# Expert-weight slots of a one-core transformer block: tiles of the front part kept as small rings, and a new order of slots

## The chip, the cores and the metric

The kernel runs on one core of a Trainium2 chip. The metric is device time in microseconds of one execution. Three timed runs of the kernel before took 698.36, 703.17 and 704.9 us, so the median is 703.17 us. The profiled execution took 699.28 us, of which 697.5 us lie between the first and the last instruction.

## The reference

One block over 256 tokens of width 1024. A normalised and modulated input goes through one projection into three mixers (an RWKV-7 recurrence, differential attention, block attention), their outputs through `w_out`, and the sum is added to `x`. Then comes a mixture of 32 experts with two levels of routing:

```
mod = cs @ ada_w + ada_b                      # 6 x 1024 modulation vectors
h   = rmsnorm(x, norm1_g) * (1 + sc1) + sh1
y_r, y_d, y_m = three mixers of (h @ w_in)
x   = x + g1 * (concat(y_r, y_d, y_m) @ w_out)
h2  = rmsnorm(x, norm2_g) * (1 + sc2) + sh2
# each token: best of 4 groups, then 2 of its 8 experts
x   = x + g2 * sum over chosen experts e of gate * (silu(h2 @ w1[e]) * (h2 @ w3[e])) @ w2[e]
```

All arrays are float32. The experts' weights are 32 x 3 x 2 MB = 201 MB. They are all read, whatever the routing.

## The kernel before

**Order of the work.** The front part (modulation, projections, mixers, `w_out`) comes first. The router follows, and then nine groups of experts: group 0 is experts 0 to 3, known beforehand; the numbers of the others come from a permutation `perm` that the router computes. For each group, `hidden` gathers the tokens, multiplies by `w1` and `w3` (output `h`), and `experts_out` multiplies by `w2` (output `yb`).

**Loads.** Every load is issued by SP, in one queue in order. `wtile` (L1173) hands out a place of 1 MB for each load of expert weights: a full expert takes two for `w1`, two for `w3`, two for `w2`, so there are 192 such tiles, 24 of them for group 0. In a group the order of tiles is first halves of `w1`, first halves of `w3`, second halves of `w1`, second halves of `w3`, then `w2`. L1170 sets from which ring each place is taken, and the list is gone through again and again; it has 20 places. I number the tiles 1 to 192 in that order; tile 21 takes the place of tile 1, and its load waits until TensorE has used tile 1 up. Tile 21 still belongs to group 0. SP's queue reaches `perm` (L1190) behind tile 24.

**Places.** `ringB` holds ten tiles. In the front part they are four tiles of `w_in` (`wR`), the recurrence's operands (KB, MA, ER, ta), `dqk` and `tb`; two of them are taken again for half of `w_out` (`rwo`). `ringA` holds two tiles (modulation and projection weights, later the other half of `w_out`). `ringC` holds eight, and is opened only when the pools of the front part are closed (L985 to L988). So tiles 1 to 12 go into places that come free within the front part, and 13 to 20 into `ringC`.

**Other tiles of the front part.** `ringF` (two places) holds the modulation weights (`ra`); its last four loads, `in_adaM`, are used by matmuls `ga`, which make the gate `g2`. The transposed input `hT` and the split weights `wp1` share one place, `wp0` has one of its own, and `hTl` and the mixers' output `mT` share another. All of these lie in the pool `fr`, which closes with the front part. The projection's matmuls `pt` are the last that read `wp0` and `wp1`.

**What sets the order.** The program is laid out by a scheduler that simulates it and places each instruction in its engine's queue when its operands and its place are there by the simulation. It also sets the order of SP's queue, within the order that `load_next` fixes for the front part's own loads.

Of the kernel before, what the change touches and what calls it, by code (L numbers as in the profile page):

```python
# [8 lines left out]
FT = mybir.dt.float32  # L9
FR = mybir.dt.float32r  # L10
# [8 lines left out]
S, D, NT = 256, 1024, 2  # L19
# [3 lines left out]
BIG = 1.0e30  # L23


NA, NB, NC, NF = 2, 10, 8, 2
PK, GROUPS = {}, {}


# [65 lines left out]
def build(tc, ctx, a):  # L95
# [4 lines left out]
    const = ctx.enter_context(tc.tile_pool(name="const", bufs=1))  # L100
    keep = ctx.enter_context(tc.tile_pool(name="keep", bufs=1))
    ringA = ctx.enter_context(tc.tile_pool(name="ringA", bufs=NA))
    dram = ctx.enter_context(tc.tile_pool(name="dram", bufs=1, space=bass.MemoryType.DRAM))
    small = ctx.enter_context(tc.tile_pool(name="small", bufs=2))
    front = ExitStack()
    fr = front.enter_context(tc.tile_pool(name="front", bufs=1))
    ringF = front.enter_context(tc.tile_pool(name="ringF", bufs=NF))
    att = ExitStack()
    at = att.enter_context(tc.tile_pool(name="att", bufs=1))
    rp = att.enter_context(tc.tile_pool(name="rwkv", bufs=1))  # L110
    ringB = ctx.enter_context(tc.tile_pool(name="ringB", bufs=NB, side="right", reuse_waits="tile"))
# [96 lines left out]
    def ahead(it, n):  # L208

        q = []  # L210
        for x in it:
            q.append(x)
            if len(q) > n:
                yield q.pop(0)
        yield from q
# [3 lines left out]
    A.activation(cs, c_("c"), AF.Silu)  # L219
    A.activation(csb, csb, AF.Silu)  # L220

    hT = fr.tile([128, 8, S], FT, name="hT", tag="hT")
    ssx = const.tile([128, NT], FT, name="ssx")
    rx = const.tile([128, NT], FT, name="rx")
    for t in range(NT):
# [69 lines left out]
    def pieces(specs):  # L295
        for i, s_ in enumerate(specs):
            for k, w in load_win(i, s_[1] - s_[0]):
                yield s_, k, w
# [3 lines left out]
    DM = ((896, 1408, dq[:, :, 0:512], 0), (1408, 1920, dq[:, :, 512:1024], 8), (1920, 2432, dv, None),  # L302
          (2432, 2944, mqk, 16), (2944, 3200, mv, None))

    wp = [fr.tile([128, 2, 2, 512], FR, name="wp0"), None]

    def split(it):

        for x, (s_, k, w) in enumerate(it):
            if x == 2:  # L310
                wp[1] = fr.tile([128, 2, 2, 512], FR, name="wp1", tag="hT")
            hi, lo = (wp[x // 2 % 2][:, x % 2, q, :w.shape[-1]] for q in range(2))
            A.copy(hi, w)  # L313
            V.tensor_sub(lo, w, hi)  # L314
            yield s_, k, hi, lo

    hTh = keep.tile([128, 8, S], FR, name="hTh", tag="xn")
    hTl = fr.tile([128, 8, S], FR, name="hTl", tag="hTl")
    src = ahead(split(ahead(pieces(DM), 6)), 2)


# [178 lines left out]
    mt_ = []  # L500

    def mT():

        if not mt_:
            assert 2944 in done
            mt_.append(fr.tile([128, 8, S], FT, name="mT", tag="hTl"))
        return mt_[0]


# [10 lines left out]
    def rwkv():  # L520
# [222 lines left out]
        for j in range(2):  # L743
            A.activation(yr[:, j, :], pz[:, j].rearrange("p n t -> p (n t)"), AF.Identity, bias=c_("lnb")[:, j:j + 1],
                         scale=c_("lng")[:, j:j + 1])
        V.tensor_add(yr, yr, bon)
        V.tensor_mul(mT()[:, 0:2, :], yr, zg.rearrange("p (j t) -> p j t", j=2))
        done.add(("j", 0))
        done.add(("j", 1))
# [87 lines left out]
    def apply_M(i, aTs):  # L837
        po = bankt("pm_")[:, :256]
        for x, aT in enumerate(aTs):
            h = 2 * (i - 4) + x  # L840
            q = HQ[x]
            vh = mv[:, :, 64 * h:64 * h + 64]
            T.matmul(po[q, 0:128], vh[:, 0, :], aT[:, 0, :], start=True, stop=True, tile_position=(0, 64 * x))
            T.matmul(po[q, 128:256], vh[:, 0, :], aT[:, 1, :], start=True, stop=False, tile_position=(0, 64 * x))
            T.matmul(po[q, 128:256], vh[:, 1, :], aT[:, 2, :], start=False, stop=True, tile_position=(0, 64 * x))
        A.copy(mT()[:, 2 + i, :], po)

    def out_D(h2):

        rd = at.tile([128, 2, NT], FT, name="rd", bufs=2)  # L850
        rstd_of(rd.rearrange("p h t -> p (h t)"), ssd[:, 2 * h2:2 * h2 + 2, :].rearrange("p h t -> p (h t)"), 128, 1e-6,
                [128, 4])
        for t in range(NT):
            o3 = od[:, t, 256 * h2:256 * h2 + 256].rearrange("p (h e) -> p h e", h=2)
            V.tensor_mul(o3, o3, rd[:, :, t:t + 1].to_broadcast([128, 2, 128]))
        yield 0.6
        p = bankl("od").rearrange("p (h t q) -> p h t q", h=2, t=NT)
        for hh in range(2):
            h = 2 * h2 + hh
            for t in range(NT):  # L860
                T.transpose(p[:, hh, t, :], od[:, t, 128 * h:128 * h + 128], ident)
        j = slice(2 + 2 * h2, 4 + 2 * h2)
        pq = p.rearrange("p h t q -> p h (t q)")
        A.activation(mT()[:, j, :], pq, AF.Copy, scale=sub)
        done.add(("j", 2 + 2 * h2))
        done.add(("j", 3 + 2 * h2))
# [121 lines left out]
    ringC = ctx.enter_context(tc.tile_pool(name="ringC", bufs=NC, reuse_waits="tile"))  # L988
# [178 lines left out]
        A.copy(grow, pg.rearrange("p c t q -> p c (t q)"))  # L1167


    seq = [ringB] * NB + [ringA] * NA + [ringC] * NC  # L1170
    cnt = [0]

    def wtile():  # L1173
# [298 lines left out]
```

## Time and profile before

| what | value |
|---|---|
| median of three runs | 703.17 us |
| profiled execution | 699.28 us |
| its span | 697.5 us |
| TensorE busy | 582.4 us (84%) |
| VectorE busy | 255.7 us (37%) |
| moved by DMA | 249.36 MB, mean 358 GB/s |
| TensorE's mean granted clock | 0.946 |

The busy shares are averages over a front part of some 230 us, in which TensorE and VectorE have the work, and the experts' part after it, in which the same 16 DMA engines move almost nothing but expert weights. A busy TensorE in that second part includes matmuls whose ends are modelled, so the DMA row is read beside it.

### The profile page before, as it was taken

What the parts mean: (1) busy time and instruction counts of PE and PEld (TensorE: products, weight loads), DVE (VectorE), ACT (ScalarE), POOL (GpSimd) and SP (SyncE); (2) the same over time, 40 slices, a digit from 0 to 9 for tenths busy, and PEclk for the clock granted to TensorE, in tenths of its full rate; (3) what the DMA queues carried; (4) which work ended last, traced back from release to release, by engine and by line L of the source; (5) the groups of instructions that cost most, each with busy time, mean ns of one, the idle gap of its engine ahead of it and who ended that gap; (6) DMA issues with size and microseconds to landing.
All of it is one profiled execution on the core that took longest, in us unless ns stands there. A gap on an engine that the chain in (4) does not pass through costs nothing. (4 is left out here: it accounts for less than half of the span.)

```text
span 697.5 us, 9345 instructions
## 1 busy us (share of the span) xinstructions
PE 582.4 (84%) x3612; PEld 271.3 (39%) x3612; DVE 255.7 (37%) x683; ACT 135.1 (19%) x299; POOL 28.1 (4%) x39
## 2 busy tenths in 40 slices
PE   2967999999989697998867999996886688788676
PEld 1856887675444543433213243431221115121112
DVE  5777998667535742321301122130030013002002
ACT  3366444544331412101001010100000002000000
POOL 2223200000000000000000000000000000000000
PEclk9997999999989898999989999998998999899799
DMA  9991775477665699999999999999999999999996
GB/s 356 422 356 64 295 278 184 152 295 275 235 231 191 264 420 419 421 419 420 422 419 420 424 420 420 420 420 422 420 419 422 419 409 420 420 420 421 420 389 235
DMA packets 42678, 249.36 MB, mean 358 GB/s; under 512 B 4220, under 2 KB 10244, under 8 KB 14984
## 3 DMA queue, kind: packets, MB, share of 16 engines
q1 hardware_dynamic: 42632, 248.74, 88.5%
q8 instruction: 29, 0.48, 0.3%
q14 instruction: 17, 0.14, 0.1%
HBM read 247.66 MB, written 1.06 MB: 357 GB/s over the span
## 5 line engine op out<-in xcount | busy, mean ns | idle before, releaser
L69 PE MATMUL h<-rmoe,xT 128*32 128x512 f32 (+1 forms) x1024 | 191.3, 662 | 39.3 <-DMA rmoe<-in_moe_w 39.3
L69 PE MATMUL yb<-rmoe,aTm 128*32 128x512 f32 (+2 forms) x544 | 104.2, 579 | 14.2 <-DMA rmoe<-in_moe_w 9.9
L69 PEld LDWEIGHTS h<-rmoe,xT 128*32 128x32 f32 (+1 forms) x1024 | 44.2, 122 | 171.5 <-issue 90.5
L1256 DVE TENSOR_TENSOR ac<-ac,h 128x512 f32<-128x512 f32 x9 | 6.2, 688 | 168.3 <-PE h L69 167.7
L69 PEld LDWEIGHTS yb<-rmoe,aTm 128*32 128x32 f32 (+1 forms) x544 | 28.6, 113 | 82.8 <-issue 41.9
L1255 ACT ACTIVATE ac<-h 128x512 f32<-128x512 f32 x9 | 5.4, 597 | 255.2 <-PE h L69 255.1
L1291 DVE TENSOR_TENSOR yb<-yb,g2b 128x512 f32<-128x512 f32 (+1 forms) x19 | 12.6, 664 | 110.7 <-PE yb L69 110.7
L69 PE MATMUL pt<-wp,hTh 128*128 128x512 f32 (+1 forms) x160 | 51.3, 400 | 1.0 <-ACT wp L313 0.5
L69 PE MATMUL cb<-yb,ST 128*128 128x512 f32 (+1 forms) x76 | 40.3, 618 | 7.6 <-DVE x L1295 6.2
L69 PE MATMUL gx<-S,xn 128*128 128x128 f32 x288 | 40.3, 297 | 5.0 <-DVE S L85 2.2
L1295 DVE TENSOR_TENSOR x<-x,cb 128x512 f32<-128x512 f32 (+1 forms) x38 | 25.1, 660 | 50.6 <-PE cb L69 50.5
L69 PEld LDWEIGHTS gx<-S,xn 128*128 128x128 f32 x288 | 37.0, 207 | 15.6 <-issue 13.1
L1237 ACT ACTIVATE xT<-gx,sh,s2c 128x128 f32<-128x128 f32 x36 | 16.0, 456 | 94.1 <-DVE xT L1239 94.1
L69 PEld LDWEIGHTS pt<-wp,hTh 128*128 128x128 f32 x160 | 28.8, 195 | 9.3 <-issue 1.7
L69 PE MATMUL pt<-wp,hTl 128*128 128x512 f32 (+1 forms) x80 | 30.3, 381 | 0.0
L69 PE MATMUL op<-rwo,mT 128*128 128x512 f32 x64 | 30.3, 617 | 0.0
L313 ACT CAST wp<-rwin 128x512 fp32r<-128x512 f32 (+1 forms) x40 | 22.7, 576 | 29.3 <-PE pt L69 28.2
L69 PE MATMUL pr<-hT,rwin 128*128 128x256 f32 x112 | 25.2, 383 | 3.7 <-ACT hT L372 3.7
L314 DVE TENSOR_TENSOR wp<-rwin,wp 128x512 fp32r<-128x512 f32 (+1 forms) x40 | 26.5, 683 | 3.9 <-ACT wp L313 3.8
L69 PEld LDWEIGHTS cb<-yb,ST 128*128 128x128 f32 x76 | 11.6, 188 | 36.2 <-DVE x L1295 21.2
L1239 DVE TENSOR_SCALAR xT<-gx,s2c,sh 128x128 f32<-128x128 f32 x36 | 14.4, 408 | 27.3 <-PE gx L69 27.3
L69 PEld LDWEIGHTS pr<-hT,rwin 128*128 128x128 f32 x112 | 21.0, 191 | 7.8 <-ACT hT L372 4.9
(370 smaller groups left out, 558.8 us busy)
## 6 DMA issues: line engine op xcount, KB each, us to landing
rmoe<-in_moe_w SPq DMA_DIRECT2D x184, 1024.0 KB, 19.8
ra<-in_adaB SPq DMA_DIRECT2D x8, 1024.0 KB, 13.9
ra<-in_adaC SPq DMA_DIRECT2D x8, 1024.0 KB, 7.0
rwin<-in_winD SPq DMA_DIRECT2D x8, 1024.0 KB, 5.1
ra<-in_adaM SPq DMA_DIRECT2D x8, 1024.0 KB, 7.1
rwo<-in_w_out SPq DMA_DIRECT2D x4, 1024.0 KB, 8.0
rmoe<-in_moe_w SPq DMA_DIRECT2D x8, 512.0 KB, 17.1
rmoe<-in_moe_w SPq DMA_DIRECT2D x16, 256.0 KB, 5.7
```

Of the source, the lines that this page charges most:

```text
L69: return self._turn(self.engine.matmul(*ar, **kw))
L313: A.copy(hi, w)
L314: V.tensor_sub(lo, w, hi)
L1237: A.activation(xT[:, k, :], p[kk_ // 2][:, kk_ % 2, :], AF.Identity, bias=sh2[:, k:k + 1], scale=s2c[:, k:k + 1])
L1239: V.tensor_scalar(xT[:, k, :], p[kk_ // 2][:, kk_ % 2, :], s2c[:, k:k + 1], sh2[:, k:k + 1], op0=OP.mult, op1=OP.add)
L1255: A.activation(ac, hs[0], AF.Silu)
L1256: V.tensor_mul(ac, ac, hs[1])
L1291: V.tensor_mul(yb_[:, f], py_[c], g2b[:, f])
L1295: V.tensor_add(x2[:, t, f], x2[:, t, f], p)
```

## The change

The places of `hT`, `wp1` and `wp0` become `ringE` (two places), those of `hTl` and `mT` become `ringD` (one place), and `ringF` is moved out of the pools that close with the front part. All three rings stay open to the end, so the experts' tiles can use them. `ringC` shrinks from eight places to three, so there are still 20 places. The list that `wtile` goes through is written in another order: two of `ringB`, the two of `ringE`, the two of `ringF`, six of `ringB`, three of `ringC`, two of `ringA`, two of `ringB`, one of `ringD`. The diff, without its comments and blank lines:

```
-NA, NB, NC, NF = 2, 10, 8, 2
+NA, NB, NC, ND, NE_, NF = 2, 10, 3, 1, 2, 2
...
     ringA = ctx.enter_context(tc.tile_pool(name="ringA", bufs=NA))
+    ringD = ctx.enter_context(tc.tile_pool(name="ringD", bufs=ND))
+    ringE = ctx.enter_context(tc.tile_pool(name="ringE", bufs=NE_))
+    ringF = ctx.enter_context(tc.tile_pool(name="ringF", bufs=NF))
...
-    ringF = front.enter_context(tc.tile_pool(name="ringF", bufs=NF))
...
-    hT = fr.tile([128, 8, S], FT, name="hT", tag="hT")
+    hT = ringE.tile([128, 8, S], FT, name="hT", tag="r")
...
-    wp = [fr.tile([128, 2, 2, 512], FR, name="wp0"), None]
+    wp = [ringE.tile([128, 2, 2, 512], FR, name="wp0", tag="r"), None]
...
-                wp[1] = fr.tile([128, 2, 2, 512], FR, name="wp1", tag="hT")
+                wp[1] = ringE.tile([128, 2, 2, 512], FR, name="wp1", tag="r")
...
-    hTl = fr.tile([128, 8, S], FR, name="hTl", tag="hTl")
+    hTl = ringD.tile([128, 8, S], FR, name="hTl", tag="r")
...
-            mt_.append(fr.tile([128, 8, S], FT, name="mT", tag="hTl"))
+            mt_.append(ringD.tile([128, 8, S], FT, name="mT", tag="r"))
...
-    seq = [ringB] * NB + [ringA] * NA + [ringC] * NC
+    seq = [ringB] * 2 + [ringE] * NE_ + [ringF] * NF + [ringB] * 6 + [ringC] * NC + [ringA] * NA + [ringB] * 2 + [ringD] * ND
```

SP's queue behind the load of `pkC`, in the kernel before (`ra` from `in_adaM` are the gate's weights, `rmoe` the experts' tiles):

```order
L339 DMA ra<-in_adaM 128x2048
L1202 DMA rmoe<-in_moe_w 128x2048 x2
L339 DMA ra<-in_adaM 128x2048 x2
L1202 DMA rmoe<-in_moe_w 128x2048
L339 DMA ra<-in_adaM 128x2048
L1202 DMA rmoe<-in_moe_w 128x2048 x21
L1190 TENSOR_LOAD perm
```

and in the changed kernel:

```order
L342 DMA ra<-in_adaM 128x2048
L1206 DMA rmoe<-in_moe_w 128x2048 x4
L342 DMA ra<-in_adaM 128x2048 x2
L1206 DMA rmoe<-in_moe_w 128x2048
L342 DMA ra<-in_adaM 128x2048
L1206 DMA rmoe<-in_moe_w 128x2048 x19
L1194 TENSOR_LOAD perm
```

Two more loads of experts stand ahead of the last three of the gate's weights. Up to `perm` there are 24 loads of experts in both.

The end of the first round of places in SP's queue of the changed kernel. Names rise by two from tile to tile within `w1` and `w3` (`rmoe_2215` is tile 1, `rmoe_2245` tile 16) and again within `w2` (`rmoe_2413` is tile 17, `rmoe_2421` tile 21). 2245 and 2413 go into `ringA`, 2415 and 2417 into the two places of `rwo` in `ringB`, 2239 to 2243 into `ringC`, 2419 into `ringD`, and 2421 is the first that takes a used place.

```order
L1206 DMA rmoe_2237<-in_moe_w1 128x2048
L1206 DMA rmoe_2245<-in_moe_w3 128x2048
L1206 DMA rmoe_2413<-in_moe_w2 128x2048
L1206 DMA rmoe_2415<-in_moe_w2 128x2048
L1206 DMA rmoe_2239<-in_moe_w3 128x2048
L1206 DMA rmoe_2241<-in_moe_w3 128x2048
L1206 DMA rmoe_2243<-in_moe_w3 128x2048
L1206 DMA rmoe_2417<-in_moe_w2 128x2048
L1206 DMA rmoe_2419<-in_moe_w2 128x2048
L1206 DMA rmoe_2421<-in_moe_w2 128x2048
```

The same stretch in the kernel before, where 2230 and 2232 go into `ringA`, 2226 and 2228 into the places of `rwo`, the eight from 2234 to 2414 into `ringC`, and 2416 is the first that takes a used place:

```order
L1202 DMA rmoe_2230<-in_moe_w1 128x2048
L1202 DMA rmoe_2232<-in_moe_w1 128x2048
L1202 DMA rmoe_2226<-in_moe_w1 128x2048
L1202 DMA rmoe_2228<-in_moe_w1 128x2048
L1202 DMA rmoe_2234<-in_moe_w3 128x2048
L1202 DMA rmoe_2236<-in_moe_w3 128x2048
L1202 DMA rmoe_2238<-in_moe_w3 128x2048
L1202 DMA rmoe_2240<-in_moe_w3 128x2048
L1202 DMA rmoe_2408<-in_moe_w2 128x2048
L1202 DMA rmoe_2410<-in_moe_w2 128x2048
L1202 DMA rmoe_2412<-in_moe_w2 128x2048
L1202 DMA rmoe_2414<-in_moe_w2 128x2048
```

Behind the place of `rwo` that is read last there were eight loads into fresh places; now there is one, that of `ringD`.

TensorE's queue at the gate's matmuls, before:

```order
L69 MATMUL ga<-ra,cs 32x512 x4
L69 MATMUL pY<-S,MA 64x64 x2
L69 MATMUL zg<-lo,pkB 128x256 x2
L69 MATMUL lg<-kT,qT 128x128
L69 MATMUL pU<-R,tq_185 64x64 x4
L69 MATMUL op<-rwo,mT 128x512 x4
L69 MATMUL ga<-ra,cs 32x512 x4
L69 MATMUL lg<-kT,qT 128x256
```

and in the changed kernel:

```order
L69 MATMUL pY<-S,MA 64x64 x2
L69 MATMUL zg<-lo,pkB 128x256 x2
L69 MATMUL ga<-ra,cs 32x512 x4
L69 MATMUL lg<-kT,qT 128x128
L69 MATMUL pU<-R,tq_191 64x64 x4
L69 MATMUL op<-rwo,mT 128x512 x4
L69 MATMUL lg<-kT,qT 128x256
L69 MATMUL ga<-ra,cs 32x512 x4
```

The gate's matmuls stand one or two instructions later. Up to this place, and from `prb` to the end of group 0's `h`, TensorE's queue has the same instructions in the same order.

## Rows read from the trace of the kernel before

**Rows 1.** The page, part 2: GB/s in 40 equal slices of 17.4 us.

```profile
GB/s 356 422 356 64 295 278 184 152 295 275 235 231 191 264 420 419 421 419 420 422 419 420 424 420 420 420 420 422 420 419 422 419 409 420 420 420 421 420 389 235
```

**Rows 2.** The page, part 4: the chain that ended last, by line.

```profile
DMA rmoe<-in_moe_w 16%; PE h L69 1%; PE cb L69 0%; PE yb L69 0%; DVE x L1295 0%; SPq L1212 0%; SPq L1202 0%; SPq L1190 0%; DVE yb L1291 0%
```

**Rows 3.** Stages; columns: stretch, length, busy by engine, TensorE clock, DMA share, GB/s.

```profile
150.00:231.00 81.00, 75.36 (x572) 42.92 (x572) 45.46 (x158) 26.62 (x82) 0.53 (x2) 0.96 0.64 236
231.00:255.00 24.00, 18.44 (x144) 12.21 (x143) 17.87 (x86) 8.07 (x13) 0.00 (x0) 0.79 0.95 382
255.00:690.00 435.00, 360.54 (x1874) 119.37 (x1873) 74.85 (x157) 27.87 (x55) 0.00 (x0) 0.95 1.01 417
```

**Rows 4.** SP's queue in order of time: start, length to last issue, line, operation, count.

```profile
151.11 0.92 SPq L1202 DMA_DIRECT2D rmoe<-in_moe_w  x2
157.75 15.32 SPq L339 DMA_DIRECT2D ra<-in_adaM  x2
174.83 0.33 SPq L1202 DMA_DIRECT2D rmoe<-in_moe_w  x1
177.62 0.33 SPq L339 DMA_DIRECT2D ra<-in_adaM  x1
185.27 142.91 SPq L1202 DMA_DIRECT2D rmoe<-in_moe_w  x53
```

**Rows 5.** One us each around the front part's end; columns as in rows 3.

```profile
232.00:233.00 1.00, 1.00 (x10) 0.91 (x9) 0.94 (x3) 1.00 (x2) 0.00 (x0) 1.00 0.77 115
233.00:234.00 1.00, 1.00 (x12) 1.00 (x11) 0.86 (x4) 1.00 (x3) 0.00 (x0) 1.00 0.85 246
234.00:235.00 1.00, 1.00 (x12) 1.00 (x11) 0.82 (x6) 0.77 (x2) 0.00 (x0) 1.00 0.86 360
235.00:236.00 1.00, 1.00 (x12) 1.00 (x11) 0.72 (x5) 1.00 (x1) 0.00 (x0) 1.00 1.00 418
```

**Rows 6.** SP's queue, windows from 231.4, 236.6, 250.5 and 254 us.

```profile
231.53 26.43 SPq L1202 DMA_DIRECT2D rmoe<-in_moe_w  x17
...
236.71 0.33 SPq L1202 DMA_DIRECT2D rmoe<-in_moe_w  x1
...
250.57 7.39 SPq L1202 DMA_DIRECT2D rmoe<-in_moe_w  x8
...
254.01 3.96 SPq L1202 DMA_DIRECT2D rmoe<-in_moe_w  x4
```

**Rows 7.** SP's waits over the whole run: what for, us in total, times, longest.

```profile
SPq L1202 <- DMA rmoe<-in_moe_w: 286.5, 150, 3.0
...
SPq L1202 <- PE h L69: 15.2, 13, 10.6
```

**Rows 8.** TensorE in order of time: group 0's first `h`.

```profile
246.46 7.53 PE L69 MATMUL h<-rmoe,xT 128*32 128x512 f32 x64
```

**Rows 9.** The tile `rmoe`: from issue to landing.

```profile
DMA to landing us min/median/max: 5.2/19.8/20.7
```

**Rows 10.** TensorE in order of time: the last matmul that reads `wp`.

```profile
152.81 0.28 PE L69 MATMUL pt<-wp,hTl 128*128 128x256 f32 x1
```

**Rows 11.** Two us each; columns as in rows 3.

```profile
168.00:170.00 2.00, 2.00 (x28) 1.09 (x26) 0.93 (x7) 1.70 (x6) 0.00 (x0) 1.00 0.14 49
170.00:172.00 2.00, 2.00 (x25) 1.14 (x24) 1.52 (x3) 0.85 (x2) 0.00 (x0) 1.00 0.00 0
...
194.00:196.00 2.00, 1.60 (x13) 1.08 (x15) 1.27 (x5) 0.69 (x1) 0.00 (x0) 0.50 0.91 381
```

**Rows 12.** TensorE in order of time: the gate's last three matmul groups.

```profile
176.50 1.06 PE L69 MATMUL ga<-ra,cs 128*32 128x512 f32 x8
...
183.04 1.07 PE L69 MATMUL ga<-ra,cs 128*32 128x512 f32 x8
...
186.34 1.06 PE L69 MATMUL ga<-ra,cs 128*32 128x512 f32 x8
```

**Rows 13.** TensorE's waits between 150 and 232 us: the longest.

```profile
PE od L72 <- DVE dqk L855: 2.9, 1, 2.9
```

## The prediction

> **What bounds the kernel now.** I read the page's slices first. In the slices from 244 us on, the DMA engines move 419 to 424 GB/s almost without a break; before, in the front part, 64 to 295 [rows 1]. The chain that ended last is expert weights and little else: of the part that it covers, 16% of the span is a load of `rmoe`, 1% a matmul [rows 2]. The stages say the same: 417 GB/s at full DMA share over 435 us, but 236 GB/s over the 81 us before the front part's end [rows 3]. So the time is the moment from which the DMA engines run without a break, plus the bytes that are then still to come. A tile of 1.049 MB takes 2.49 us at 421 GB/s.
>
> SP's queue and the finest windows then show where that moment lies. Within the front part twelve tiles are loaded, as their places come free: two at 151, one at 174.8, the rest from 185 us on [rows 4]. The twelfth is issued at 231.53 us, when the second tile of `rwo` in `ringB` has been used, and tiles 13 to 20 follow up to 236.71, into `ringC` [rows 6]. From 232 us on these nine run; in the first three us 0.72 MB move, then 418 GB/s [rows 5]. Nine tiles are 9.44 MB; the other 8.72 MB take 20.7 us, so tile 20 ends at about 255.7. Tile 21 is issued at 250.57 [rows 6], when TensorE's first `h` (from 246.46 [rows 8]) has used tile 1 up; SP waits 10.6 us for that, the longest of 13 such waits [rows 7]. Yet it has no cost: tile 21 has its turn only at 255.7. From there on SP waits for landings, 150 times [rows 7], so no place is missing.
>
> **The change, part by part.**
>
> *The places of `ringE`, `ringF` and `ringD` in the list.* There are 20 places as before, and tile 21 still waits for tile 1. What changes is how many of the 20 are filled ahead of the front part's end. By SP's order, eighteen are issued ahead of the place of `rwo` that is read last, against eleven: behind it stands only the place of `mT`. Two tiles of `ringE` are issued behind the last matmul on `wp`, which starts at 152.81 [rows 10]. Those seven more tiles need 17.5 us of DMA time. There is room: 81 us at 236 GB/s [rows 3] leave 81 x (421 - 236) / 421 = 35.6 us of it. So at 232 us two tiles are left (2.10 MB), done at 235 + (2.10 - 0.72) / 0.421 = 238.3 us.
>
> *What is late next.* The DMA engines then stand still, since all 20 places are full, until tile 21 is issued at 250.57. What its restart costs, no row shows at that place. The nearest is the start at 231.53: 3.47 us after the issue 0.72 MB had moved [rows 5, 6]. I take that: 0.72 MB by 254.04, then 421 GB/s. In the kernel before, at 254.04, 0.70 MB of tile 20 were still to come (1.66 us x 0.421). The changed kernel is 1.42 MB ahead, **3.4 us**. The bounds: a restart without any cost gives 255.7 - 250.57 = 5.1 us; if `h` starts late, the gain shrinks by as much, below zero too.
>
> The Trainium skill, DMA: Bandwidth & Descriptors, section Anatomy of one DMA, fits a lone DMA with some 2.0 us plus bytes over 436 GB/s, for another path of issue. By that estimate tile 21 would land 4.4 us after its issue; the shortest landing here took 5.2 us [rows 9], so by the page's figure the restart is 0.8 us cheaper and the gain 4.2 us.
>
> *Whether the lead lasts.* Tiles 21 to 24 are issued between 250.57 and 254.01, tile 25 at 254.01 [rows 6] (eight issues from 250.57, four from 254.01, all done at 257.96). Each gives 2.49 us of work, so four cover 10 us, and the next four are there before the first end. The second half of group 0's `h` then frees eight more. After that the stage at 417 GB/s is as before: same bytes, same number of places, and loads that wait for landings. The 3.4 us stay to the end.
>
> *Loads ahead of the gate's weights.* Two tiles now stand ahead of the last three loads of `in_adaM`; 5.0 us of transfers. Before, the engines fall idle at about 168.3 and stay so until after 172 [rows 11]; they now work through that gap. The gate weights issued at 157.75 land up to 5.0 us later, near 173.5; their matmuls stand at 176.50, and one or two instructions later in the new order [rows 12]. The weights issued at 172.7 (the second of the two in that row) and 177.62 [rows 4] queue behind at most that same remainder, and their matmuls start at 183.04 and 186.34. I cost this at nothing; the cover is some 3 us at the first of them. Without it, everything behind on TensorE is later by up to 5.0 us, `h` included.
>
> This speaks against the change, and a page does too: the Trainium skill, DMA: Bandwidth & Descriptors, section Queues, rings and completion order, says that each DMA engine takes the descriptors of a ring in order, so an early tile can't be overtaken. The trace agrees, as far as a median landing of 19.8 us [rows 9], eight tiles of 2.49 us, shows a queue served in turn.
>
> *SP's own queue.* A load that waits for its place holds up what stands behind it. Tiles 5 and 6 wait for the last two gate matmuls, from 184 and 187 us on; behind them are only experts' tiles. Nothing that TensorE reads before 246 us is behind one of those waits. Cost: nothing.
>
> *The new rings themselves.* `hT`, `wp`, `hTl` and `mT` share places exactly as before. `ringC`'s three tiles need no more memory than its eight. Cost: nothing. The reordered gate matmuls and the additions on VectorE that follow them move within 1 us, beside a wait of 2.9 us for VectorE [rows 13]; I bound that at 1 us either way and take zero.
>
> **The sum.** 699.28 - 3.4 = 695.9 us against the profiled execution; 703.17 - 3.4 = 699.8 against the median. The four executions shown have a mean of 701.4, and from there I get **698 us**.
>
> **Rivals.**
>
> *Nothing gained.* Were the early loads not early on the chip, because one place in SP's queue comes free late (tile 5 behind a gate matmul, say), up to nine tiles would be left at 232 us as before. For it: SP takes its queue in order, and half a dozen waits stand ahead. Against it: each of those waits ends by 231 us in the trace of before, with idle DMA time behind it. Result 699.3 against the profile, 701.4 by the mean. Chance 0.18.
>
> *Slower.* A gate matmul waits for its weights and holds up the whole of TensorE behind it. It decides from a landing after 176.5 us. Price: up to 5.0 us of waiting, and a clock that falls: TensorE's granted clock is 0.50 at 194 to 196 us [rows 11], shortly behind the wait of 2.9 us [rows 13], that is 1.2 GHz in place of 2.4. Ten us of such a stretch cost up to 5 more. `h` then starts 10 us later, and so does tile 21: -3.4 + 10 = +6.6, 708.0 by the mean. For it: the cover is only 3 us. Against it: of TensorE's waits from 150 to 232 us none is for a load; the longest is that for VectorE. Chance 0.11.
>
> *Faster by over 1%.* The additions of the gate now stand behind some of the softmax work on VectorE. If that takes away the wait of 2.9 us [rows 13] and the low clock behind it (about 5 us at half speed, some 2.5 us), `h` starts 5.4 us earlier and the gain is 8.8 us: 692.6 by the mean. Against it: VectorE has the same work to do ahead of the row that TensorE waits for. Chance 0.11.
>
> The forecast has the other 0.60.
>
> **Range and chances.** A measurement of this kernel can tell about 1% (7 us) from no change; its own three runs lie 6.5 us apart. From the fastest run less the upper bound, 698.36 - 5.1 = 693.3, to the slowest run with nothing gained, 704.9; I stretch the low end a little into the faster rival: 692 to 705. That leaves out most of the slower rival and half of the faster one. A gain of 3.4 us is 0.5%, so the forecast and the first rival lie within 1% but for the scatter of the runs, to which I give 0.10 on the faster side and 0.01 on the other. Faster by over 1% 0.21, within 1% 0.68, slower 0.11.
>
> **What would show it.** In the profile of the changed kernel: four loads of `rmoe` by 154 us and none of `in_adaM` later than before; two issues or so of `rmoe` after 231; idle DMA engines from about 238 until tile 21 is issued; the first `h` at 246.5, within 1 us; tile 21 at 250.6. After it 417 GB/s without a gap, and a span of 694.1 us. The prediction is wrong if the first `h` moves by more than 2 us, if the DMA engines work through from 232 to 255 as before, or if a gap appears after tile 24.

## The result: 0.9907 of the time before, and the profile after

The changed kernel takes 693.67 us (median of nine runs, 691.64 to 697.15) against 702.35 us (nine runs, 698.36 to 704.9) of the kernel before: a ratio of **0.9907, interval 0.9882 to 0.9933**. That is some 6.5 us; I had forecast 3.4. (The two medians lie 8.7 us apart; single runs scatter by 5 to 7 us, and the text goes by the ratio.) The profiled executions say nearly the same: 693.48 us with a span of 691.7, against 699.28 and 697.5.

The changed kernel's stages, with a last row of 360 us that lies wholly in the experts' part (columns as in [rows 3]):

```profile
150.00:231.00 81.00, 75.79 (x571) 43.10 (x571) 45.01 (x158) 26.72 (x82) 0.53 (x2) 0.96 0.80 308
231.00:255.00 24.00, 18.45 (x140) 11.79 (x138) 18.03 (x86) 8.07 (x13) 0.00 (x0) 0.79 0.48 189
300.00:660.00 360.00, 293.23 (x1467) 91.97 (x1465) 58.54 (x121) 19.97 (x41) 0.00 (x0) 0.97 1.01 423
```

The last of these for the kernel before:

```profile
300.00:660.00 360.00, 295.75 (x1449) 93.00 (x1452) 58.60 (x120) 18.46 (x38) 0.00 (x0) 0.95 1.01 420
```

Two things differ. From 150 to 231 us the DMA engines move 308 GB/s in place of 236 [rows 3], 5.8 MB more, and rest in the next 24 us (189 GB/s against 382). And in the experts' part, at the same full DMA share, they move 423 GB/s where they moved 420. I had expected the first alone.

SP's queue of the changed kernel in order of time, beside [rows 4], and its issues around the front part's end, beside [rows 6]:

```profile
151.09 2.36 SPq L1206 DMA_DIRECT2D rmoe<-in_moe_w  x4
157.72 15.32 SPq L342 DMA_DIRECT2D ra<-in_adaM  x2
174.79 0.33 SPq L1206 DMA_DIRECT2D rmoe<-in_moe_w  x1
178.77 0.33 SPq L342 DMA_DIRECT2D ra<-in_adaM  x1
...
222.41 3.13 SPq L1206 DMA_DIRECT2D rmoe<-in_moe_w  x4
231.71 0.81 SPq L1206 DMA_DIRECT2D rmoe<-in_moe_w  x2
251.11 0.80 SPq L1206 DMA_DIRECT2D rmoe<-in_moe_w  x2
```

Four tiles go out by 154 us, the gate's loads hardly later (the last of them by 1.2 us); only two tiles are left at 231.71, and then nothing until tile 21 at 251.11. In windows (columns as in [rows 3]), beside [rows 5] and [rows 11], the engines first fill the old gap at 168 to 172 us, then stand still for some eleven:

```profile
168.00:170.00 2.00, 2.00 (x28) 1.12 (x26) 0.90 (x7) 1.73 (x6) 0.00 (x0) 1.00 0.99 418
170.00:172.00 2.00, 2.00 (x23) 1.10 (x23) 1.56 (x3) 0.82 (x2) 0.00 (x0) 1.00 1.05 430
...
238.00:240.00 2.00, 0.00 (x0) 0.00 (x0) 1.73 (x12) 0.94 (x1) 0.00 (x0) 0.52 0.77 320
240.00:242.00 2.00, 0.30 (x5) 0.19 (x4) 1.79 (x12) 0.00 (x0) 0.00 (x0) 0.50 0.06 25
242.00:252.00 10.00, 9.03 (x60) 4.97 (x64) 8.99 (x37) 1.68 (x7) 0.00 (x0) 0.68 0.00 0
252.00:253.00 1.00, 1.00 (x12) 0.24 (x8) 0.00 (x0) 0.00 (x0) 0.00 (x0) 1.00 0.91 172
253.00:254.00 1.00, 1.00 (x16) 0.24 (x8) 0.00 (x0) 0.00 (x0) 0.00 (x0) 1.00 0.87 303
254.00:255.00 1.00, 1.00 (x13) 0.55 (x5) 0.00 (x0) 0.00 (x0) 0.00 (x0) 1.00 0.98 418
```

TensorE's gate matmuls, then the first matmuls of group 0, beside [rows 12] and [rows 8]:

```profile
177.64 1.06 PE L69 MATMUL ga<-ra,cs 128*32 128x512 f32 x8
183.69 1.06 PE L69 MATMUL ga<-ra,cs 128*32 128x512 f32 x8
187.44 1.07 PE L69 MATMUL ga<-ra,cs 128*32 128x512 f32 x8
...
242.97 3.76 PE L69 MATMUL gx<-S,xn 128*128 128x128 f32 x16 [2.24 <-DVE S L85]
246.65 7.87 PE L69 MATMUL h<-rmoe,xT 128*32 128x512 f32 x64
```

And SP's waits over the whole run (what for, us in total, times, longest), beside [rows 7]:

```profile
SPq L1206 <- DMA rmoe<-in_moe_w: 268.5, 143, 2.7
...
SPq L1206 <- PE h L69: 25.0, 13, 18.6
```

SP's longest wait for `h` has grown from 10.6 to 18.6 us and is no longer hidden. The chain of work is still expert weights: 17% of the span, everything else under 1%, as in [rows 2].

### The profile page after: what moved, and what is told of

It reads as the page before. It is cut to its first block, busy times and chain, and to the rows that moved or that the text cites. A ratio compares the mean times of both kernels' runs of the same rounds, so it can differ in the third digit from the quotient of the medians.

```text
span 691.7 us, 9348 instructions
## 1 busy us (share of the span) xinstructions
PE 575.7 (83%) x3612; PEld 269.2 (39%) x3612; DVE 255.1 (37%) x683; ACT 135.1 (20%) x299; POOL 27.1 (4%) x39
## 5 line engine op out<-in xcount | busy, mean ns | idle before, releaser
L69 PE MATMUL h<-rmoe,xT 128*32 128x512 f32 (+1 forms) x1024 | 188.2, 642 | 42.0 <-DMA rmoe<-in_moe_w 41.9
L69 PE MATMUL yb<-rmoe,aTm 128*32 128x512 f32 (+2 forms) x544 | 100.7, 573 | 13.2 <-DMA rmoe<-in_moe_w 8.8
L367 DVE CUSTOM_DVE_ANT_0 ra<-ra,mqk,bs 128x1024 f32<-128x1024 f32 x16 | 23.3, 1459 | 0.0
```

What stands on the lines that cost most here:

```text
L69: return self._turn(self.engine.matmul(*ar, **kw))
L367: last["V"] = V.tensor_tensor_reduce(f, f, csb, 1.0, start, OP.mult, OP.add, to)
```

## The experiments

The questions were: how much of the gain is the earlier loading and how much the faster stream; is the faster stream a matter of one execution or of where the places lie in memory; and what now sets the start of the stream.

Two quantities are taken from the records of single DMA packets. *Packet* is the mean duration of an 8 KB packet (one partition's row of an expert tile), over some 15,000 of them between 288 and 588 us. *Lead* is how much earlier than in the kernel before, counted from the span's start, the first 72 MB had moved; that falls just behind the restart (266.5 us in the kernel before). *Front end* is the end of the last `op` matmul, the last that reads `rwo`, and *from it* is the lead counted from there. The start address of each place in its partition is read from the built program, as the offset past a multiple of 256 bytes.

| kernel | places at offset 0 / 192 / 224 | packet, ns | front end, us | lead, us | from it, us | span, us | ratio to before, interval |
|---|---|---|---|---|---|---|---|
| before | 2 / 0 / 18 | 314.6 | 231.5 | 0 | 0 | 697.5 | 1 |
| before_again | 2 / 0 / 18 | 314.7 | 230.1 | 1.5 | 0.1 | 695.7 | 1.0032 [1.0013, 1.0051] |
| changed | 7 / 0 / 13 | 312.5 | 231.7 | 3.1 | 3.2 | 691.7 | 0.9907 [0.9882, 0.9933] |
| after_again | 7 / 0 / 13 | 312.6 | 231.8 | 3.2 | 3.5 | 691.7 | 0.9910 [0.9891, 0.9930] |
| hold | 7 / 0 / 13 | 312.3 | 234.4 | -2.5 | 0.4 | 697.2 | 0.9966 [0.9944, 0.9987] |
| oldlist | 7 / 0 / 13 | 312.5 | 229.9 | 5.1 | 3.5 | 689.7 | 0.9902 [0.9876, 0.9928] |
| a_warm | 7 / 0 / 13 | 312.6 | 232.7 | 1.0 | 2.2 | 693.8 | 0.9928 [0.9901, 0.9955] |
| b_warm | 2 / 0 / 18 | 314.7 | 234.8 | -3.2 | 0.0 | 700.5 | 0.9989 [0.9971, 1.0006] |
| a_al | 0 / 20 / 0 | 314.5 | 232.0 | 2.8 | 3.2 | 694.8 | 0.9947 [0.9927, 0.9968] |
| b_al | 0 / 20 / 0 | 314.5 | 231.3 | 0.3 | 0.2 | 697.2 | 0.9993 [0.9977, 1.0009] |
| a_mis | 0 / 0 / 20 | 315.6 | 231.3 | 3.7 | 3.4 | 695.6 | 0.9974 [0.9954, 0.9994] |
| a_al_warm | 0 / 20 / 0 | 314.5 | 232.0 | 5.1 | 5.6 | 692.5 | 0.9935 [0.9915, 0.9955] |

All columns but the last and the places are of one execution each; the ratios are of many runs. The front part's own length varies between executions (before_again has a lead of 1.5 us without any change), and counting from its end takes that out: the early loads by themselves give 3.2 to 3.5 us, and the kernels without them stand at 0.0 to 0.4. Every span in the table follows from packet and lead within 0.5 us: 697.5 less the lead, less 430 us (the stream's length) times the packet's saving over 314.6. For the changed kernel 697.5 - 3.1 - 430 x 2.1 / 314.6 = 691.5, measured 691.7. This tells where in the span the time lies; what causes the two terms is for the experiments.

**Both kernels again.** No edit.

> The changed kernel once more, with a second profile. The lead that the DMA engines have by 277 us was 2.6 us in its first profile; from there to the end it grew to 5.4 us, since they moved 422 to 424 GB/s in place of 419 to 421. Theory A (the lead is the change; the rate belongs to the execution): the rate between 300 and 540 us lies anywhere between 419 and 424 GB/s in this profile, and the gain in time is about 3 us. Theory B (the places of the tiles in memory set the rate): the rate is 422 to 424 GB/s again, and the gain is 6 us again.

> The kernel before once more, with a second profile. Theory A (the rate belongs to the execution): between 300 and 540 us it can be other than the 420 to 421 GB/s of its first profile. Theory B (the places in memory set it): 420 to 421 GB/s again. Both: tile 20 ends near 255.7 us, tile 21 is issued near 250.6.

Measured: the same gain, and the same 312.6 and 314.7 ns. The faster stream belongs to the program, not to the execution.

**The changed places without the lead (hold).** The rings of the change, with tiles 13 to 20 kept behind tiles 1 to 12 in SP's queue:

```
-    seq = [ringB] * 2 + [ringE] * NE_ + [ringF] * NF + [ringB] * 6 + ...
+    seq = [ringB] * NB + [ringA] * NA + [ringC] * NC + [ringE] * NE_ + [ringF] * NF + [ringD] * ND
...
+                if cnt[0] <= 12:
+                    early.append(ins)
+                elif cnt[0] <= 20:
+                    for x in early:
+                        behind(ins, x)
```

> The changed kernel's rings and memory, but the eight loads into the places of ringC, ringE, ringF and ringD stand behind the twelve into ringB and ringA in SP's queue, so that only twelve tiles are loaded within the front part, as before. Theory A (early loads make the lead, nothing else is changed): the DMA engines run without a break from 232 us, tile 20 ends at 255.7, and the time is that of the kernel before within 1 us. Theory B (the places in memory set the rate): 423 GB/s after 300 us, and some 3 us faster than before without any lead.

Measured: 696.73 us, ratio 0.9966, some 2.4 us, with the DMA engines at work through the whole of 238 to 254 us:

```profile
238.00:242.00 4.00, 1.88 (x17) 1.78 (x17) 3.01 (x20) 3.56 (x2) 0.00 (x0) 0.83 1.01 422
242.00:250.00 8.00, 4.57 (x25) 3.88 (x28) 7.58 (x35) 1.22 (x6) 0.00 (x0) 0.50 1.01 427
```

So without the early loads a part of the gain is still there. The front part of its profiled execution ended 2.9 us later than in the kernel before; that is the lead of -2.5, and counted from the front part's end 0.4 is left.

**The changed rings with a list in the old order (oldlist).** The first line of that edit alone.

> The changed kernel's rings, but the list of places in the order of the kernel before: ten of ringB, two of ringA, three of ringC, then ringE, ringF, ringD. If the order of the list sets what is loaded early: tiles in the new rings are loaded last, about eight tiles are left at 232 us, and the lead of some 3 us is gone. If the scheduler loads whatever place is free first, whatever its rank in the list: SP's queue has eighteen tiles ahead of the last place of rwo, as in the changed kernel, and the time is that of the changed kernel within 1 us.

Measured: 691.74 us, 0.9902, not distinguishable from the change. Four tiles go out from 150.26 us here too:

```profile
150.26 2.23 SPq L1206 DMA_DIRECT2D rmoe<-in_moe_w  x4
156.54 15.31 SPq L342 DMA_DIRECT2D ra<-in_adaM  x2
```

What makes the early loads possible is that the three rings outlive the front part. The order of the list adds nothing that these runs can tell, since the scheduler places each load in SP's queue when its place is free.

**Matmuls that keep TensorE's clock up, first attempt (a_warm, b_warm).** Ahead of `h` TensorE waits 3.3 us for VectorE and then runs `gx` at a granted clock of 0.50, the lower of its two levels. Eleven extra matmuls (128x512, float32), whose output nobody reads, were to keep it at 1.00, in the changed kernel and in the one before; seven stand ahead of `prk`, the matmuls that wait those 3.3 us, and four between `prk` and `gx`:

```
+    w1_ = warm(7, rl_[0])
...
+    w2_ = warm(4, pk_)
```

> The changed kernel with eleven extra matmuls (128x512, results unread) on TensorE where it waits for the router: seven ahead of prk, four between prk and gx. They keep TensorE busy between 237 and 243 us, where it waits for VectorE and its granted clock falls to 0.50 until 248.6 us. Theory A (the first h now sets when tile 21 is issued, and so the end): gx and the first h run at full clock, h starts about 1.9 us earlier (near 244.8), tile 21 is issued about 3 us earlier (near 248), and the time falls by about 3 us against the changed kernel. Rival (the gap of the DMA engines costs nothing at the end, because the lead is lost later): no change against the changed kernel.

> The same eleven matmuls in the kernel before. Theory A: h starts about 1.9 us earlier here too and tile 21 is issued earlier, but tile 20 ends at 255.7 us whatever TensorE does, so the time stays that of the kernel before within 0.5 us. Rival (an earlier h is worth time by itself): as much faster as in the changed kernel.

Mis-sized: each of them left two records, and the eleven took 9.9 us, where I had counted half. TensorE of a_warm:

```profile
237.92 6.26 PE L69 MATMUL warm<-x,pkA 128*128 128x512 f32 x14
...
244.14 3.68 PE L69 MATMUL warm<-x,pkA 128*128 128x512 f32 x8
247.65 1.95 PE L69 MATMUL gx<-S,xn 128*128 128x128 f32 x16
249.53 4.93 PE L69 MATMUL h<-rmoe,xT 128*32 128x512 f32 x44
```

`gx` did run in 1.95 us in place of 3.76, but `h` came 2.9 us later, tile 21 2.1 us later (253.18), and the span was 2.1 us longer. Of each of these 1.0 us is a front part that ended later, ahead of all the extra matmuls, so these cost `h` 1.9 us and tile 21 1.1, and 1.0 to 1.3 of the lead counted from the front part's end is gone. The last `op` matmuls, first of the changed kernel, then of a_warm:

```profile
227.97 3.70 PE L69 MATMUL op<-rwo,mT 128*128 128x512 f32 x8
228.95 3.70 PE L69 MATMUL op<-rwo,mT 128*128 128x512 f32 x8
```

In the kernel before, `h` came 5.2 us later (251.66), 3.3 of it from the front part (its last `op` matmuls from 231.07 in place of 227.80) and again 1.9 from the extra matmuls. Its lead counted from the front part's end is 0.0, and the time of many runs did not change (0.9989); its DMA engines had not been idle:

```profile
244.00:250.00 6.00, 6.00 (x21) 2.80 (x20) 3.55 (x17) 0.76 (x5) 0.00 (x0) 1.00 1.01 423
250.00:254.00 4.00, 4.00 (x40) 2.35 (x42) 3.97 (x13) 0.91 (x2) 0.00 (x0) 1.00 1.01 418
```

A miss as a gain, but it tells the two kernels apart: the same 1.9 us on `h` are free before the change, and after it cost what they delay tile 21 by.

**A place less (a_nc2, b_nc7).** `NC` 3 to 2 in the changed kernel, 8 to 7 in the one before; 19 places in each.

> The changed kernel with two places in ringC in place of three: nineteen places in all. Theory A (all places are full before h starts, and the DMA engines then stand still): one tile fewer is in place when they stop, near 238.5 us in place of 241, tile 20 waits for h as tile 21 does now, and the time rises by one tile, 2.5 us, against the changed kernel. Rival (places are not what is short): no change.

> The kernel before with seven places in ringC in place of eight: nineteen places in all. Theory A: eight tiles are left at 232 us, the last ends near 253.2 us, and the next is issued at 250.6 when h has used tile 1 up, so the DMA engines still have no break: same time as before within 0.5 us. Rival (every place is worth a tile of time, early or late): 2.5 us slower.

Measured: 706.06 us, 1.0097 [1.0065, 1.013], and 708.15 us, 1.0121 [1.0084, 1.0159]. Both theories missed these times, for a reason elsewhere: at the `If` of `overflow` (L1306, L1302 in the kernel before) SP waits for TensorE's queue, 14.0 us in a_nc2 and 13.0 in b_nc7, against 7.3 in the changed kernel and 2.3 in the one before. With 20 places the tiles in flight cover that; with 19 the engines run dry. Windows and wait of a_nc2:

```profile
560.00:565.00 5.00, 3.83 (x18) 0.79 (x20) 0.00 (x0) 0.00 (x0) 0.00 (x0) 1.00 0.79 303
565.00:570.00 5.00, 4.22 (x16) 1.03 (x8) 2.07 (x3) 0.00 (x0) 0.00 (x0) 1.00 0.02 7
570.00:575.00 5.00, 2.60 (x5) 0.59 (x4) 2.17 (x4) 0.00 (x0) 0.00 (x0) 1.00 0.01 3
```

```profile
SPq L1206 <- PEq L1306: 14.0, 1, 14.0
```

The stall comes some 300 us behind the start of the stream, which can be read by itself, and there the first theory of each holds. In a_nc2 the DMA engines stop by 238 us and tile 20 goes out only at 249.27, together with tile 21; the lead counted from the front part's end is 1.1 us, 2.1 to 2.4 less than with 20 places, about one tile. In b_nc7 it is 0.0, and the engines have no break. Issues and windows of a_nc2, then a window of b_nc7:

```profile
249.27 0.80 SPq L1206 DMA_DIRECT2D rmoe<-in_moe_w  x2
...
238.00:240.00 2.00, 0.29 (x5) 0.18 (x4) 1.79 (x11) 0.00 (x0) 0.00 (x0) 0.50 0.00 0
240.00:250.00 10.00, 8.63 (x60) 4.91 (x64) 9.33 (x40) 1.68 (x7) 0.00 (x0) 0.69 0.00 0
```

```profile
240.00:250.00 10.00, 7.75 (x57) 4.68 (x60) 9.68 (x40) 1.68 (x7) 0.00 (x0) 0.66 1.02 425
```

**Where the places start (a_al, b_al, a_mis).** By then I held that a packet is faster into a place that starts at a multiple of 64 bytes: in the changed kernel's list the seven places of `ringA`, `ringD`, `ringE` and `ringF` took some 310 ns, the thirteen of `ringB` and `ringC`, 32 bytes past such a multiple, some 315. a_al and b_al put all 20 places at multiples of 64, a_mis, with its pads ahead of `ringA` and behind `ringF`, puts all of them 32 past; rings, list and work stay.

```
+    padB = ctx.enter_context(tc.tile_pool(name="padB", bufs=1, side="right"))
+    V.memset(padB.tile([128, 8], FT, name="padB_"), 0.0)
...
-    qg = const.tile([128, 2], FT, name="qg")
+    few = const.tile([128, 8], FT, name="few")
+    qg = few[:, 0:2]
...
```

> The changed kernel with every one of its 20 expert places starting at a multiple of 64 bytes in the partition (7 of 20 do so in the changed kernel, 2 of 20 in the kernel before). Two pads of 32 bytes are added, and three small constants share one tile. Theory (the start address of a place sets the packet's time): the mean 8 KB packet of the expert stream takes about 309.5 ns in place of 312.5, 1.0% of some 430 us, so 4.4 us less than the changed kernel: about 689 us, a ratio of 0.985 to the kernel before. Rival (it is which ring or which end of the memory, not the address's last bits): packets stay at 312.5 ns, 693 us, ratio 0.991.

> The kernel before, with its rings and list, and only the same pads: all 20 places at a multiple of 64 bytes in place of 2. Theory: packets about 309.5 ns in place of 314.6, 1.6% of some 430 us, about 7 us less than before without any earlier load: about 692 to 693 us, ratio 0.990; tile 21 issued at about 250.5 us as before. Rival (address does not matter): packets 314.6 ns, ratio 1.00.

> The changed kernel with all 20 places moved to 32 bytes past a multiple of 64. Theory: packets about 315 ns in place of 312.5, about 3 us more than the changed kernel: about 696.5 us, ratio 0.9965; what is left of the gain is the earlier loading alone. Rival: 312.5 ns, ratio 0.991.

Measured, over the same 360 us, first a_al, then b_al, then a_mis:

```profile
300.00:660.00 360.00, 294.46 (x1467) 93.86 (x1465) 58.53 (x121) 19.83 (x41) 0.00 (x0) 0.97 1.01 420
```

```profile
300.00:660.00 360.00, 294.83 (x1460) 93.14 (x1464) 58.58 (x120) 18.48 (x38) 0.00 (x0) 0.96 1.01 420
```

```profile
300.00:660.00 360.00, 293.57 (x1458) 91.73 (x1456) 57.82 (x120) 19.16 (x40) 0.00 (x0) 0.96 1.01 419
```

The theory in my form fell: with all places at multiples of 64 the changed kernel lost its fast stream, and the kernel before gained none. The rival fell with it, since the seven places are still the same rings at the same end of the memory, moved by 64 bytes, and their packets went from some 310 to 314 ns. What fits all kernels is the offset within 256 bytes. To make room for the pads I had merged three small constants, and that moved the seven places from offset 0 to 192. By place, averaged over tiles whose neighbours in the list have the same offset: 309.6 ns at offset 0 (18 tiles of hold), 314.1 at 192 (114 tiles of a_al), 315.1 at 224 (114 tiles of a_mis). The front part's loads of 8 KB rows between 3 and 33 us show it too: 309.6 ns in the changed kernel, where all their places are at offset 0, 313.5 in a_al, where all are at 192.

The places don't simply add up, though. Seven at 309.6 and thirteen at 315.1 would make 313.2 ns, and the changed kernel has 312.5; against the 314.6 of the kernel before, this accounts for 1.4 of the 2.1 ns. The rest lies with tiles at 224 that stand beside tiles at 0. Between 290 and 550 us, 56% of hold's packets took 309 ns to the nanosecond, where seven places of 20 and the 7% that a_mis has of such packets would make 40%. Why a neighbour gains is not shown.

The Trainium skill, DMA: Bandwidth & Descriptors, section How a descriptor splits into AXI transactions, says that a transaction starts at a multiple of 256 bytes, so that a descriptor with another start pays for the bytes below it too. By its beats of 32 bytes, an estimate, an 8 KB row would cost 262 at offset 192 and 263 at 224 in place of 256, 2.3 and 2.7% more. The runs agree in direction and order, and show 1.5 and 1.8%; that section of the Trainium skill speaks of reads, and here it is the written side whose address changes.

Two of these kernels also give the lead by itself. a_al and b_al have the same packets (314.5 ns) and differ by the change alone: 696.5 against 698.95 us, spans 694.8 and 697.2, 2.4 us by either; the front part of a_al ended 0.6 us later, and counted from there it is some 3 us.

**The extra matmuls, resized (a_al_warm).** a_al with three ahead of `prk` and two behind it.

> The kernel with all places at a multiple of 64 bytes, and five extra 128x512 f32 matmuls, three ahead of prk and two between prk and gx, which compute nothing that is used. The earlier run with eleven came late because each took two passes. Theory (in the changed kernel the first h sets when tile 21 is issued, and so the end): gx runs at full clock in about 1.95 us in place of 3.8, the first h starts 1 to 2 us earlier, tile 21 is issued 2 to 3 us earlier, and the time is 2 to 3 us less than that of the kernel with the pads alone: about 686.5 us. Rival (the earlier release is lost again in the transfer stream, or the extra matmuls cost what they give): no difference from the kernel with the pads alone.

Measured: 694.23 us against 696.5 of a_al (12 and 11 runs; the means differ by 1.5 us, with an interval of 0.3 to 2.6 by drawing from these runs again), spans 692.5 and 694.8. TensorE and SP of a_al_warm:

```profile
243.25 2.16 PE L69 MATMUL gx<-S,xn 128*128 128x128 f32 x16 [0.45 <-DVE S L85]
245.34 7.08 PE L69 MATMUL h<-rmoe,xT 128*32 128x512 f32 x64
```

```profile
249.00 0.33 SPq L1224 DMA_DIRECT2D rmoe<-in_moe_w  x1
```

and of a_al:

```profile
243.23 3.75 PE L69 MATMUL gx<-S,xn 128*128 128x128 f32 x16 [2.24 <-DVE S L85]
246.91 7.88 PE L69 MATMUL h<-rmoe,xT 128*32 128x512 f32 x64
```

```profile
251.38 0.80 SPq L1211 DMA_DIRECT2D rmoe<-in_moe_w  x2
```

`h` starts 1.6 us earlier, tile 21 goes out 2.4 us earlier, and the span is 2.3 us shorter, at the low end of what I had put down. So after the change, TensorE's way to the first `h` sets the start of the stream, and through it the end. The extra matmuls on the changed kernel with its own addresses, and a kernel with all 20 places at offset 0, were not run; by 309.6 against 312.5 ns the second would be some 4 us faster than the change (0.9% of 430), an estimate.

## Why the prediction was right, and where it was short

- *What bounds the kernel*: right. Time is the start of the unbroken stream plus its bytes; the spans of all twelve executions of the table follow from these two.
- *The early places*: right. Four loads by 154 us, two issues after 231 us, idle engines until tile 21. They stopped between 239 and 241 us, not at 238.3: of the seven more tiles, 5.8 MB had moved by 231 us, not 7.3. Since the engines then rest, that cost nothing.
- *The restart*: right in size. 0.72 MB had moved at 254.59, 3.48 us after tile 21's issue; I had taken 3.47. The estimate from the Trainium skill (DMA: Bandwidth & Descriptors, Anatomy of one DMA), 0.8 us cheaper, did not come about.
- *The lead*: right. It is 3.1 us for 3.4, and 3.2 to 3.5 counted from the front part's end. Tile 21 went out at 251.11, 0.54 us later than in [rows 6], since `h` began 0.19 us later and its 64 matmuls took 7.87 us in place of 7.53 [rows 8]; that leaves 2.9 of the 3.4. The clock is 0.50 from 246 to 248 us here, 0.64 in the kernel before. My bound "if `h` starts late, the gain shrinks by as much" is what a_warm and a_al_warm show from both sides, by the issue of tile 21: 1.1 us later there, 2.4 earlier here.
- *Whether the lead lasts*: right; a_al against b_al 2.5 us at 72 MB, 2.4 at 248 MB.
- *Loads ahead of the gate's weights, SP's queue*: right in size. The last gate load goes out 1.2 us later, against the sign that none would; the gate's matmuls come 1.1 us later at most, none waits for a load, and the 2.9 us for VectorE [rows 13] became 2.8. So neither the slower rival nor the one by over 1% came about, and "nothing gained" fell with the windows.
- *The step that failed*: "The new rings themselves", costed at nothing, and with it "After that the stage at 417 GB/s is as before". I counted places and bytes, and not where the places start. Five more of the 20 at offset 0 give, with what their neighbours gain, 2.1 ns of 314.6, 2.9 us over the stream; hold shows 2.4 us by its ratio, a_al, which takes them away, 2.6 (0.9947 less 0.9910). That is the part of the gain, nearly half, that the sum lacked. The forecast of 698 us was 4.3 above the 693.67 measured; 2.9 of that is this term, and the rest is within the scatter of single runs. The sign and the mechanism of the lead stood, the size of the gain was half. That the range held the result is in part its width, 13 us, since it had no term for this.
- *The chances*: by the scatter that the text states, the forecast and the first rival leave 0.67 within 1% and 0.12 slower, not 0.68 and 0.11; nothing hangs on it.

What stays open: whether an offset of 128, or of 64, is as good as 0 (no place of the experts has one in these kernels), why tiles at 224 beside tiles at 0 are faster too, and why the front part ends up to 5 us apart in single executions (229.9 to 234.8 us).

## What to carry to other kernels

When a kernel is bound by its transfer stream, read the start of the stream and its rate apart, and see after an edit which instruction now releases the first load of the stream: here a wait that had been free became the bound. A change of pools changes addresses: list where the destinations start before costing "the same places, elsewhere" at nothing. And an experiment that moves one thing in memory moves its neighbours; look at all the addresses that it gives, and not only at those that it means.

## What the runs showed of the hardware

- An 8 KB packet into a place at a multiple of 256 bytes took 309.6 ns, at 192 past it 314.1, at 224 past it 315.1: 1.5 to 1.8%, visible in the time of a kernel that streams for 430 us. Where both kinds stand side by side, a part of the packets at 224 took 309 ns as well.
- An `If` behind a count that is read at run time held SP's queue for 13 to 14 us with 19 places and 2.3 to 7.4 with 20; with 19 the DMA engines ran dry behind it, for 8.9 us in a_nc2 and 6.4 in b_nc7.
- The DMA stream paid its restart after eleven idle us with 3.5 us for the first 0.72 MB, just as after the front part.
